# Layer 1's output projection split over heads: three heads' share moved among the attention heads, the rest kept behind them

## The chip, the cores and the metric

The kernel runs on one core of a Trainium2 chip. Its engines work side by side, each through its own queue in order: TensorE (PE; its weight loads are listed as PEld), VectorE (DVE), ScalarE (ACT), GpSimd (POOL) and SyncE (SP), the last of which only issues transfers (DMAs); GpSimd issues some too. The metric is the device time of one launch in microseconds: the median of several runs, and beside it one execution under the profiler, whose trace is quoted.

## What is computed

One inference step of a two-layer decoder trunk: 1024 prompt tokens (16 meta tokens ahead of them) and 8 running sequences of one token each. Layer 0 is a gated linear attention, layer 1 a differential attention over 8 heads; an MLP with squared ReLU follows each, and each result goes through a LayerNorm with a scaled residual. This document is about the end of layer 1's attention. In the reference, cut to that:

```python
def diff_core(q, k, v, q_pos, k_pos, lam):
    s = jnp.einsum('bqhmd,bkhmd->bhmqk', q, k).astype(F32) * (DIFF_DH ** -0.5)
    ...
    p = jax.nn.softmax(s, axis=-1)
    a = p[:, :, 0] - lam * p[:, :, 1]
    return jnp.einsum('bhqk,bkhe->bqhe', a, v.astype(F32))

def diff_output(o, g_sub, lam_init, w_out, dtype):
    B, T = o.shape[:2]
    o = rms_norm(o, g_sub) * (1.0 - lam_init)
    return o.reshape(B, T, DIFF_HEADS * DIFF_DV).astype(dtype) @ w_out

# in reference(), per layer
x_p = post_norm(x_p, f_p, ln_mix_g[layer], ln_mix_b[layer])   # LayerNorm of ALPHA * x + f
x_p = post_norm(x_p, sq_relu_mlp(x_p, mlp_w1[layer], mlp_w2[layer]), ln_mlp_g[layer], ln_mlp_b[layer])
```

The product with w_out sums over the 8 heads (1024 = 8 x 128), so it can be made in parts: some heads first, the others later, and both added to the residual.

## The kernel before

All float32 products of full size are made as three float32r matmuls (`mm3`, profile lines L186 to L188): each operand is split into a high part and the rest (`hi`, `lo`), and hi*hi, hi*lo and lo*hi are summed in PSUM. A weight is loaded into a buffer `raw`, its high part is made on ACT (L173) and the rest on POOL (L174). PSUM is used through three groups of buffers: `mmt` (3), `axt` (3) and `smt` (2).

Layer 1's attention is a loop over 8 heads, and in each over 8 tiles of 128 query rows. `prep(h + 1)` is issued with the first tile of head h: it loads keys, queries and values of the next head (SP), transposes them (PE, L1134 to L1144), splits them (ACT L182, DVE L183) into `XH.t` and `XL.t` of that head's parity, and moves halves between partitions with nine DMAs on POOL's queue (L1150 to L1156). `tile_` makes the scores of both maps (PE L1178 and L1179 into `mmt`; for head 0 L1174 to L1176), masks them and takes the minimum (DVE L1182), takes exps (ACT L1184), combines the two maps (DVE L1186 to L1188), transposes the result (PE L1197 into `axt`), copies it to SBUF as `aT` (ACT L1199, six buffers) and multiplies it with the values (PE L1202 into `smt`). The combined scores of a tile live in `as`, five buffers of the pool `scp`. After four tiles the outputs are copied to `Y` (L1237). `o_norm` scales finished heads (power L1213 on POOL, product L1214 on POOL or DVE).

`o_fm(h, c)` transposes a head's normalized output for rows 512c to 512c + 511 and splits it into `XH[:, h]` and `XL[:, h]` (PE L1220, ACT L1221, DVE L1222). As `XH.t` and `XL.t` hold keys and queries until the last heads, all sixteen `o_fm` come in or behind head 7: half 0 after its first four tiles (rows 0 to 511 come first there), half 1 after its last. `Y` is then loaded again from `xres` in DRAM, where the residual waits (L1261, eight DMAs on SP's queue).

`w_out` (L882) multiplies with layer 1's output weight: four units of 256 columns (`kunit`, whose buffers `whi` and `wlo` the heads use for loaded keys and values), for each half of the rows, in tiles of 2 x 128 rows and 8 heads: 2 x 8 x 3 = 48 matmuls of 128x256 a tile, 16 tiles. DVE adds each tile to `Y` (L900). The samples' part runs beside it (`samples`, issued with the fifth tile): one power on POOL (L1307), 16 products with weights loaded through five buffers `rw` (PE L506). `normalize` follows each row as soon as it is complete, and the MLP of layer 1 takes the result; its weights come through `raw`, `rw` and `RW`.

The order in which the instructions stand in each queue is set by a scheduler that works out a timeline of its own from the program and gives earlier code precedence: an instruction that is ready can be set ahead of one that is not.

Of the kernel before, what the change touches and what calls it, by code (L numbers as in the profile page):

```python
# [11 lines left out]
F32 = mybir.dt.float32  # L12
F32R = mybir.dt.float32r
# [3 lines left out]
ALU = mybir.AluOpType  # L17
# [4 lines left out]
P = 128  # L22
# [6 lines left out]
GH = 4  # L29
FF = 4096  # L30
NPG = 32
ALPHA = 4.0 ** 0.25
EPS = 1e-5
NEG = -1e30
# [76 lines left out]
def hybrid_step(ctx, tc, A, dbg=None, upto=9):  # L111
# [4 lines left out]
    def bc(ap, shape, axis):  # L116
        return ap.unsqueeze(axis).broadcast_to(shape)
# [761 lines left out]

    def w_out(w, scaled, side=None):  # L882

        units = {}
        n = 0
        for u, c in ((0, 0), (1, 0), (0, 1), (1, 1), (2, 0), (3, 0), (2, 1), (3, 1)):
            if u not in units:
                units[u] = kunit(w, u * 256)
            hv, lv = (x.rearrange("p (k n) -> p k n", n=256) for x in units[u])
            for i2 in range(2):  # L890
                ps = mmt()
                t0 = 4 * c + 2 * i2
                for i in range(2):
                    a = slice((t0 + i) * P, (t0 + i + 1) * P)
# [4 lines left out]
                if scaled:  # L899
                    V.tensor_tensor(yv, yv, pv, op=ALU.add)  # L900
                else:
                    steps_v.append(V.scalar_tensor_tensor(yv, yv, ALPHA, pv, ALU.mult, ALU.add).ins)
                if side and (n == 4 if scaled else n < 12):
# [128 lines left out]
    normalize(w_out(A["gla_w_out"][0], False, paged), stats, lambda c: to_fm(c, 0))  # L1032
    normalize(mlp(paged), stats, lambda c: to_fm(c, 1))
    e.close()
    if upto == 2:
# [56 lines left out]


    de.close()
    e = ExitStack()
    a1 = e.enter_context(tc.tile_pool(name="a1", bufs=1))
    a2 = e.enter_context(tc.tile_pool(name="a2", bufs=4))
    a3 = e.enter_context(tc.tile_pool(name="a3", bufs=6))
    scp = e.enter_context(tc.tile_pool(name="scp", bufs=5))
    CW = 448  # L1100
    cm = a1.tile([P, CW], F32, name="cmask")
    V.memset(cm[:, : CW - P], 0.0)
# [110 lines left out]
        G.tensor_tensor(r, r, bc(mhalf[:, :n], [P, n, m], 2), op=ALU.pow)  # L1213
        eng.tensor_tensor(Yd[:, ts, hs], Yd[:, ts, hs], bc(r, [P, n, m, P], 3), op=ALU.mult)  # L1214

    def o_fm(h, c):
        cs = slice(512 * c, 512 * c + 512)
        ps = axt()
        for i in range(4):
            TE.transpose(ps[:, i * P : (i + 1) * P], Yt[:, 4 * c + i, h * P : (h + 1) * P], ident)  # L1220
        S.activation(XH[:, h, cs], ps, AF.Copy, scale=gs)  # L1221
        V.scalar_tensor_tensor(XL[:, h, cs], ps, gs, XH[:, h, cs].bitcast(F32), ALU.mult, ALU.subtract)  # L1222
# [28 lines left out]
    e.close()  # L1251


# [10 lines left out]
    HF = hp.tile([P, NB, 2, TH], F32, name="HF")  # L1264

    RX = hp.tile([P, 4 * TH], F32, name="RX")
    RW = hp.tile([P, 4, 512], F32, name="RW")
# [31 lines left out]

    def samples():  # L1300

        oq = hp.tile([P, 8, NS], F32, name="zoq")
        V.tensor_tensor(oq, oT, oT, op=ALU.mult)
        ps = smt()
        TE.matmul(ps[:, :64], one, oq.rearrange("p h b -> p (h b)"), start=True, stop=True)
        V.tensor_scalar(oq.rearrange("p h b -> p (h b)"), ps[:, :64], 1.0 / P, EPS, ALU.mult, ALU.add)
        G.tensor_tensor(oq, oq, bc(mhalf, [P, 8, NS], 1), op=ALU.pow)  # L1307
        V.tensor_tensor(oq, oq, oT, op=ALU.mult)
        soT = hp.tile([P, NB, TS], F32, name="zoT")
        V.memset(soT, 0.0)  # L1310
        V.tensor_scalar(soT[:, :, NM : NM + NS], oq, gs, None, ALU.mult)
# [260 lines left out]
```

## Time and profile before

| | us |
|---|---|
| median of 3 runs | 2902.23 (2901.81 to 2903.02) |
| the profiled execution | 2897.76 |
| its span, first to last instruction | 2896.0 |
| mean granted TensorE clock | 0.981 |

In the trace head 3 of layer 1 begins at about 1898 us and the last value product of head 7 starts at 2064.3 us; the additions of w_out (L900) run from 2061.7 to 2170.5 us. Rows of the view by windows read: the window in us, its length, then busy us and number of instructions for PE, PEld, DVE, ACT and POOL, then the granted TensorE clock, the DMA engines' share and GB/s. Rows of groups read: line, engine, operation, out<-in, shapes, count, busy us and mean ns of one, then the engine's idle time just before such instructions and what ended it. Rows of the timeline read: start, duration, engine, line, operation and count, and in brackets the idle time before. A matmul's duration includes its way through the pipeline, so that those of neighbours overlap.

### The profile page before, as it was taken

How to read it: one execution, taken by the hardware profiler on the slowest of the kernel's cores; microseconds unless marked ns; L12 is line 12 of the kernel's file. 1: busy time of each engine (PE TensorE's matmuls, PEld its weight loads, DVE VectorE, ACT ScalarE, POOL GpSimd, SP SyncE). 2: the span in 40 equal slices, each digit the busy share in tenths (PEclk: the TensorE clock that was granted, in tenths of full speed). 3: DMA queues.
4: the chain of work that ended last, by engine and by line, in shares of the span. 5: the costliest groups of instructions: out<-in, count | busy, mean ns of one | idle time of the engine just before them, and what ended most of it. 6: DMA issues, size and time to landing. Idle time of an engine off the chain costs nothing. (4 is left out here: it accounts for less than half of the span.)

```text
span 2896.0 us, 52075 instructions
## 1 busy us (share of the span) xinstructions
PE 2773.3 (96%) x19653; PEld 2267.4 (78%) x19653; DVE 1882.9 (65%) x2982; ACT 1043.5 (36%) x2075; POOL 1132.4 (39%) x867
## 2 busy tenths in 40 slices
PE   8889999999999999999999999989998999999997
PEld 5666767997777777777798988888988888797985
DVE  2565544567878777778768822888538846738378
ACT  3233444252221221221231112777424535345352
POOL 1231212234333433333333321122426766777664
PEclk9899999999999999999999998999999999999998
DMA  7557651624798898898668995463447678695894
GB/s 250 181 176 261 245 177 39 231 73 145 268 350 299 301 351 303 321 323 310 254 225 302 363 341 142 101 137 82 120 132 220 174 220 222 160 287 119 258 240 88
DMA packets 285366, 636.46 MB, mean 220 GB/s; under 512 B 25510, under 2 KB 141292, under 8 KB 273852
## 3 DMA queue, kind: packets, MB, share of 16 engines
q1 hardware_dynamic: 252716, 520.66, 52.4%
q0 software_dynamic: 32400, 112.50, 16.2%
q8 instruction: 154, 2.52, 0.4%
q14 instruction: 96, 0.79, 0.1%
HBM read 575.55 MB, written 44.06 MB: 214 GB/s over the span
## 5 line engine op out<-in xcount | busy, mean ns | idle before, releaser
L174 POOL TENSOR_TENSOR wlo<-raw,whi 128x512 fp32r<-128x512 f32 x256 | 357.1, 1408 | 730.1 <-ACT whi L173 635.8
L186 PE MATMUL mmt<-whi,XH 128*128 128x256 f32 (+1 forms) x1760 | 526.1, 300 | 2.2 <-ACT Y L310 2.0
L187 PE MATMUL mmt<-wlo,XH 128*128 128x256 f32 (+1 forms) x1760 | 525.9, 299 | 0.9 <-POOL wlo L174 0.9
L186 PE MATMUL mmt<-XH,whi 128*128 128x512 f32 (+1 forms) x1216 | 436.5, 360 | 7.0 <-DVE HL L183 6.6
L188 PE MATMUL mmt<-whi,XL 128*128 128x256 f32 x1536 | 436.6, 285 | 0.5 <-DVE XL L183 0.5
L188 PE MATMUL mmt<-XH,wlo 128*128 128x512 f32 (+1 forms) x1216 | 434.3, 358 | 0.0
L173 ACT CAST whi<-raw 128x512 fp32r<-128x512 f32 x256 | 153.1, 619 | 579.5 <-PE mmt L188 206.3
L187 PEld LDWEIGHTS mmt<-wlo,XH 128*128 128x128 f32 x1760 | 332.2, 189 | 30.9 <-issue 19.0
L186 PEld LDWEIGHTS mmt<-whi,XH 128*128 128x128 f32 x1760 | 331.5, 189 | 28.2 <-issue 13.5
L790 DVE TENSOR_REDUCE sc<-pg 128x16 f32<-128x1024 f32 x256 | 309.5, 1214 | 62.5 <-POOL pg L789 59.3
L187 PE MATMUL mmt<-XL,whi 128*128 128x512 f32 x768 | 307.3, 400 | 0.0
L188 PEld LDWEIGHTS mmt<-whi,XL 128*128 128x128 f32 x1536 | 289.8, 189 | 13.5 <-issue 11.8
L789 DVE TENSOR_TENSOR pg<-pg,qb 128x1024 f32<-128x1024 f32 x192 | 263.7, 1375 | 53.4 <-DMA pg<-in_cache_k 38.2
L789 POOL TENSOR_TENSOR pg<-pg,qb 128x1024 f32<-128x1024 f32 x64 | 158.8, 2482 | 297.9 <-DMA pg<-in_cache_k 182.4
L186 PEld LDWEIGHTS mmt<-XH,whi 128*128 128x128 f32 x1216 | 230.6, 190 | 54.8 <-issue 14.6
L188 PEld LDWEIGHTS mmt<-XH,wlo 128*128 128x128 f32 x1216 | 231.0, 190 | 38.1 <-issue 5.9
L187 PE MATMUL mmt<-wlo,HH 128*128 128x512 f32 x512 | 204.7, 400 | 0.0
L188 PE MATMUL mmt<-whi,HL 128*128 128x512 f32 x512 | 204.6, 400 | 0.0
L186 PE MATMUL mmt<-whi,HH 128*128 128x512 f32 x512 | 204.4, 399 | 0.0
L187 PEld LDWEIGHTS mmt<-XL,whi 128*128 128x128 f32 x768 | 145.5, 190 | 38.3 <-issue 7.1
L1416 POOL TENSOR_TENSOR wlo<-RW,whi 128x512 fp32r<-128x512 f32 x96 | 156.7, 1762 | 37.1 <-ACT whi L1415 37.1
L1416 POOL TENSOR_TENSOR wlo<-rw,whi 128x512 fp32r<-128x512 f32 x92 | 148.8, 1690 | 43.3 <-ACT whi L1415 43.2
(441 smaller groups left out, 5745.6 us busy)
## 6 DMA issues: line engine op xcount, KB each, us to landing
pg<-in_cache_k SPq DMA_DIRECT2D x256, 512.0 KB
pg<-in_cache_v SPq DMA_DIRECT2D x256, 512.0 KB
XH<-xc POOLq DMA_DIRECT2D x42, 1032.0 KB, 8.7
raw<-in_mlp_w SPq DMA_DIRECT2D x164, 256.0 KB
swt<-in_mlp_w SPq DMA_DIRECT2D x32, 1024.0 KB
rw<-in_mlp_w SPq DMA_DIRECT2D x116, 256.0 KB
RW<-in_mlp_w POOLq DMA_DIRECT2D x96, 256.0 KB, 6.1
xc<-XH POOLq DMA_DIRECT2D x14, 1032.0 KB, 7.6
```

What stands on the lines that cost most here:

```text
L173: S.copy(hi[:, c], raw)
L174: G.tensor_tensor(lo[:, c], raw, hi[:, c].bitcast(F32), op=ALU.subtract)
L186: TE.matmul(ps, ah, bh, start=first, stop=False)
L187: TE.matmul(ps, ah, bl, start=False, stop=False)
L188: TE.matmul(ps, al, bh, start=False, stop=last)
L789: eng.tensor_tensor(pg, pg, qb, op=ALU.mult)
L790: return V.tensor_reduce(sc[:, n, :], pg.rearrange("p (h d) -> p h d", d=64), op=ALU.add, axis=AX.X).ins
L1416: G.tensor_tensor(lo[:, k, :], t, hi[:, k, :].bitcast(F32), op=ALU.subtract)
```

## The change

w_out of layer 1 is made in two parts. Heads 0 to 2 (`EH = 3`): a generator `early_out` issues, one step at a time, `o_fm` of these heads into tiles of their own (`OH`, `OL`), and then for each of the four column units and each pair of row blocks a tile of 2 x 3 x 3 = 18 matmuls, whose result ACT copies into an `aT` buffer and POOL's queue adds to `xres` in DRAM with an accumulating DMA. Its weights lie in a part of `XL.t` that the heads leave free. Steps are taken in heads 2 to 7: four in each of heads 2 to 6, two in head 7. Heads 3 to 7 remain for `late_out`, 2 x 5 x 3 = 30 matmuls a tile, for each half of the rows all four units; the weights of the first three units are split during head 7 (`late_weights`), two of them into the places of `OH` and `OL`. The reloads of `Y` from `xres` go to POOL's queue. The samples' normalization moves to the end of head 1 (`samples_in`). `as` has four buffers where it had five, and the MLP's tile `HF` is allocated only after w_out, in the place of `OH` and `OL`.

```diff
+EH = 3
...
-    scp = e.enter_context(tc.tile_pool(name="scp", bufs=5))
+    scp = e.enter_context(tc.tile_pool(name="scp", bufs=4))
...
-    def o_fm(h, c):
+    def o_fm(h, c, hi=None, lo=None):
         cs = slice(512 * c, 512 * c + 512)
+        if hi is None:
+            hi, lo = XH[:, h - EH, cs], XL[:, h - EH, cs]
...
+    def reload(c):
+        for u in range(4):
+            nc.gpsimd.dma_start(Yt[:, 4 * c : 4 * c + 4, u * 256 : (u + 1) * 256], A["xres"][512 * c : 512 * c + 512, u * 256 : (u + 1) * 256].rearrange("(t p) n -> p t n", p=P))
+    OH = ep.tile([P, EH, T], F32R, name="OH")
+    OL = ep.tile([P, EH, T], F32R, name="OL")
+    wv_ = [x.rearrange("p a n -> p (a n)")[:, 3088 : 3088 + 256 * EH] for x in XL.t]
+    def halves_of(hi, lo, k0, u):
+        for x in range(0, hi.shape[1], 512):
+            w = min(512, hi.shape[1] - x)
+            raw = wrp.tile([P, 512], F32, name="raw")
+            dma(raw[:, :w].rearrange("p (k n) -> p k n", n=256), wo[:, k0 + x // 256 : k0 + (x + w) // 256, u * 256 : (u + 1) * 256])
+            S.copy(hi[:, x : x + w], raw[:, :w])
+            G.tensor_tensor(lo[:, x : x + w], raw[:, :w], hi[:, x : x + w].bitcast(F32), op=ALU.subtract)
+    def out_tile(xh, xl, w, nk, t0):
+        hv, lv = (x.rearrange("p (k n) -> p k n", n=256) for x in w)
+        ps = mmt()
+        for i in range(2):
+            a = slice((t0 + i) * P, (t0 + i + 1) * P)
+            for k in range(nk):
+                mm3(ps[:, i * 256 : (i + 1) * 256], xh[:, k, a], xl[:, k, a], hv[:, k, :], lv[:, k, :], k == 0, k == nk - 1)
+        return ps
+    def early_out():
+        halves_of(*wv_, 0, 0)
+        for h in range(EH):
+            for c in range(2):
+                cs = slice(512 * c, 512 * c + 512)
+                o_fm(h, c, OH[:, h, cs], OL[:, h, cs])
+                yield
+        for u in range(4):
+            for t0 in range(0, 8, 2):
+                ps = out_tile(OH, OL, wv_, EH, t0)
+                o = a3.tile([P, 4, P], F32, name="aT").rearrange("p j q -> p (j q)")
+                S.copy(o, ps)
+                nc.gpsimd.dma_start(A["xres"][t0 * P : (t0 + 2) * P, u * 256 : (u + 1) * 256].rearrange("(i p) n -> p i n", p=P), o.rearrange("p (i n) -> p i n", n=256), accum_op=ALU.add)
+                if t0 == 6 and u < 3:
+                    halves_of(*wv_, 0, u + 1)
+                yield
+    def late_weights():
+        u = len(late_w)
+        if u in (1, 2):
+            x = (OH, OL)[u - 1].rearrange("p k t -> p (k t)")
+            w = x[:, :LW], x[:, LW : 2 * LW]
+        else:
+            w = [wsp.tile([P, 2048], F32R, name=x)[:, :LW] for x in ("whi", "wlo")]
+        halves_of(*w, EH, u)
+        late_w.append(w)
...
             if n == 3 and h == 7:
                 o_norm(V, slice(0, 4), slice(7, 8))
-                for j in range(8):
+                for j in range(EH, 8):
                     o_fm(j, 0)
-        if h < 6 and h % 2:
-            o_norm(G, slice(0, 8), slice(h - 1, h + 1))
-        elif h == 6:
-            o_norm(G, slice(0, 8), slice(6, 7))
+                reload(0)
+            if h == 2 and n < 4 or h == 3 and n in (0, 2, 4, 6) or 3 < h < 7 and n % 2 == 0 or h == 7 and n < 2:
+                next(early)
+            if h == 7 and n in (1, 2, 4):
+                late_weights()
+        if h == 1:
+            soT = samples_in()
+        if h in (1, 2, 4, 6):
+            o_norm(G, slice(0, 8), slice(2 if h == 2 else h - 1, h + 1))
     o_norm(V, slice(4, 8), slice(7, 8))
-    for j in range(8):
+    for j in range(EH, 8):
         o_fm(j, 1)
+    reload(1)
...
-    for c in range(2):
-        for u in range(4):
-            dma(Yt[:, 4 * c : 4 * c + 4, u * 256 : (u + 1) * 256], A["xres"][512 * c : 512 * c + 512, u * 256 : (u + 1) * 256].rearrange("(t p) n -> p t n", p=P))
...
-    normalize(w_out(A["diff_w_out"][0], True, samples()), stats, lambda c: to_fm(c, 2, xr))
+    def late_out():
+        side, n = samples(), 0
+        late_weights()
+        for c in range(2):
+            for u in range(4):
+                for t0 in (4 * c, 4 * c + 2):
+                    ps = out_tile(XH, XL, late_w[u], NB - EH, t0)
+                    yv = Yt[:, t0 : t0 + 2, u * 256 : (u + 1) * 256]
+                    V.tensor_tensor(yv, yv, ps.rearrange("p (i n) -> p i n", n=256), op=ALU.add)
+                    if n == 4:
+                        next(side)
+                    n += 1
+                    if u % 2:
+                        for t in (t0, t0 + 1):
+                            yield t, u // 2
+    normalize(late_out(), stats, lambda c: to_fm(c, 2, xr))
```

What this makes of the order, at two places. First TensorE's queue at the beginning of head 4, where the last transposes of head 5's preparation and the scores of head 4 stand. Before, scores (L1178, L1179), transposes of the combined scores (L1197) and value products (L1202) follow them:

```order
L1144 MATMUL axt<-c_ident,wlo 128x128 x4
L1178 MATMUL mmt<-XH_83 128x464
L1179 MATMUL mmt<-XH_83,XL_85 128x464
L1197 MATMUL axt<-c_ident,as 128x128 x4
L1178 MATMUL mmt<-XH_83 128x448
L1179 MATMUL mmt<-XH_83,XL_85 128x448
L1197 MATMUL axt<-c_ident,as 128x128 x5
L1202 MATMUL smt<-vm_20991,aT 128x128
L1202 MATMUL smt<-whi,aT 128x128 x3
```

Now, at the same place, in the numbering of the changed kernel, where L187 to L189 are the three matmuls of `mm3`:

```order
L1144 MATMUL axt<-c_ident,wlo 128x128 x4
L1178 MATMUL mmt<-XH_83 128x384
L1179 MATMUL mmt<-XH_83,XL_85 128x384
L187 MATMUL mmt<-XL_85,OH 128x256
L188 MATMUL mmt<-XL_86,OH 128x256
L189 MATMUL mmt<-XL_85,OL 128x256
L187 MATMUL mmt<-XL_85,OH 128x256
L188 MATMUL mmt<-XL_86,OH 128x256
L189 MATMUL mmt<-XL_85,OL 128x256
```

Of the 18 rows of that tile of early_out the first six are shown; the others follow in the same manner, without a row of the heads between them, and three more such blocks stand further back in the head.

Second, GpSimd's queue in head 4, where the moves of head 5's keys and queries stand. Before:

```order
L1154 DMA XL_86<-XL_86 64x1024
L1155 DMA XL_86<-XL_86 64x1024
L1214 TENSOR_TENSOR Y<-Y,orr 128x8x256
L1151 DMA XH_84<-XL_86 64x1040
L1156 DMA XH_84<-XH_84 64x1024
L1156 DMA XL_86<-XL_86 64x1024
```

Now (L1243 splits weights of early_out, L1267 is the accumulating DMA, L1228 the reload of `Y`):

```order
L1154 DMA XL_86<-XL_86 64x1024
L1155 DMA XL_86<-XL_86 64x1024
L1243 TENSOR_TENSOR XL_86<-raw,XL_85 128x512
L1151 DMA XH_84<-XL_86 64x1040
L1243 TENSOR_TENSOR XL_86<-raw,XL_85 128x256
L1267 DMA xres<-aT 128x2x256
L1156 DMA XH_84<-XH_84 64x1024
L1156 DMA XL_86<-XL_86 64x1024
L1267 DMA xres<-aT 128x2x256
L1228 DMA Y<-xres 128x4x256
L1267 DMA xres<-aT 128x2x256 x2
```

Weight splits, accumulating DMAs and a reload now stand between and behind the moves; the product L1214 that stood here is elsewhere.

More of the change, by code (lines that the diff above doesn't have):

```diff
@@ L878, in hybrid_step, with w_out @@
                 split(XH[:, 2 * h + m, cs], XL[:, 2 * h + m, cs], fmv[:, h, c, m, :])
-    def w_out(w, scaled, side=None):
+    def w_out(w, side):
         units = {}
@@ L898, in w_out @@
                 pv = ps.rearrange("p (i n) -> p i n", n=256)
[L899 to L903, printed above, removed]
+                steps_v.append(V.scalar_tensor_tensor(yv, yv, ALPHA, pv, ALU.mult, ALU.add).ins)
+                if n < 12:
                     next(side)
@@ L1031, in hybrid_step @@
     paged = decode()
-    normalize(w_out(A["gla_w_out"][0], False, paged), stats, lambda c: to_fm(c, 0))
+    normalize(w_out(A["gla_w_out"][0], paged), stats, lambda c: to_fm(c, 0))
     normalize(mlp(paged), stats, lambda c: to_fm(c, 1))
@@ L1094, in hybrid_step @@
     de.close()
+    ee = ExitStack()
+    ep = ee.enter_context(tc.tile_pool(name="ep", bufs=1, side="right"))
     e = ExitStack()
@@ new lines, in hybrid_step @@
+    OH = ep.tile([P, EH, T], F32R, name="OH")
+    OL = ep.tile([P, EH, T], F32R, name="OL")
+    wo = A["diff_w_out"][0].rearrange("(k p) n -> p k n", p=P)
+    wv_ = [x.rearrange("p a n -> p (a n)")[:, 3088 : 3088 + 256 * EH] for x in XL.t]
[6 more added lines that the diff above has]
+            G.tensor_tensor(lo[:, x : x + w], raw[:, :w], hi[:, x : x + w].bitcast(F32), op=ALU.subtract)
@@ new lines, in hybrid_step, with samples_in @@
+    LW = 256 * (NB - EH)
+    late_w = []
+    def late_weights():
[7 more added lines that the diff above has]
+        late_w.append(w)
+    def samples_in():
+        oq = ep.tile([P, 8, NS], F32, name="zoq")
+        V.tensor_tensor(oq, oT, oT, op=ALU.mult)
+        ps = smt()
+        TE.matmul(ps[:, :64], one, oq.rearrange("p h b -> p (h b)"), start=True, stop=True)
+        V.tensor_scalar(oq.rearrange("p h b -> p (h b)"), ps[:, :64], 1.0 / P, EPS, ALU.mult, ALU.add)
+        G.tensor_tensor(oq, oq, bc(mhalf, [P, 8, NS], 1), op=ALU.pow)
+        V.tensor_tensor(oq, oq, oT, op=ALU.mult)
+        soT = ep.tile([P, NB, TS], F32, name="zoT")
+        V.memset(soT, 0.0)
+        V.tensor_scalar(soT[:, :, NM : NM + NS], oq, gs, None, ALU.mult)
+        return soT
@@ L1225, in hybrid_step @@
+    early = early_out()
     nxt = prep(0)
@@ L1300, in samples @@
     def samples():
[L1302 to L1311, printed above, removed]
         s_post(s_rows(soT, A["diff_w_out"][0], NB), 2, hp)
@@ L1315, in hybrid_step @@
     stats = ln_stats(hp)
-    normalize(w_out(A["diff_w_out"][0], True, samples()), stats, lambda c: to_fm(c, 2, xr))
+    def late_out():
[14 more added lines that the diff above has]
+    normalize(late_out(), stats, lambda c: to_fm(c, 2, xr))
+    ee.close()
+    fp = e.enter_context(tc.tile_pool(name="fp", bufs=1))
+    HF = fp.tile([P, NB, 2, TH], F32, name="HF")
     if upto == 4:
```

5 lines of the change are left out of this document (2 added, 3 removed).

## The prediction

> **What bounds the kernel now.** I read the page's busy line first, then the stretches around the last layer-1 heads, then single instructions.
>
> ```profile
> PE 2773.3 (96%) x19653; PEld 2267.4 (78%) x19653; DVE 1882.9 (65%) x2982; ACT 1043.5 (36%) x2075; POOL 1132.4 (39%) x867
> ```
>
> 96% for TensorE is an average over stages. The windows by stage (busy us per engine, counts in brackets, then clock, DMA share, GB/s) separate them: two whole heads, the end of head 7, and the three pieces of w_out behind it.
>
> ```profile
> 1931.00:1961.00 30.00, 26.57 (x198) 23.37 (x197) 26.36 (x78) 21.15 (x53) 11.16 (x11) 1.00 0.63 133
> 1961.00:1993.00 32.00, 29.97 (x215) 27.64 (x215) 27.82 (x99) 24.28 (x58) 4.59 (x9) 0.95 0.40 93
> 2042.60:2064.60 22.00, 21.62 (x183) 21.02 (x184) 10.94 (x23) 9.43 (x19) 1.01 (x1) 1.00 0.20 62
> 2064.60:2104.70 40.10, 39.40 (x335) 39.15 (x333) 16.57 (x28) 9.32 (x16) 22.83 (x13) 1.00 0.55 150
> 2104.70:2131.10 26.40, 26.40 (x133) 14.19 (x131) 2.66 (x4) 3.09 (x5) 7.51 (x6) 1.00 0.61 187
> 2131.10:2171.30 40.20, 40.20 (x343) 40.20 (x343) 22.58 (x53) 15.52 (x20) 8.53 (x9) 1.00 0.30 101
> ```
>
> From 2042.6 to 2171.3 TensorE is busy 127.6 of 128.7 us while VectorE works 52.8. All of w_out lies there (3 x 256 = 768 records), and VectorE's additions wait for it:
>
> ```profile
> L186 PE MATMUL mmt<-whi,XH 128*128 128x256 f32 x256 | 72.4, 286 | 0.2 <-ACT XH L1221 0.2
> L187 PE MATMUL mmt<-wlo,XH 128*128 128x256 f32 x256 | 72.4, 284 | 0.0
> L188 PE MATMUL mmt<-whi,XL 128*128 128x256 f32 x256 | 72.2, 285 | 0.0
> ...
> L900 DVE TENSOR_TENSOR Y<-Y,mmt 128x512 f32<-128x512 f32 x16 | 11.0, 685 | 48.1 <-PE mmt L188 48.1
> ```
>
> In the heads both engines look 85 to 90% busy, but a matmul's 284 ns overlap its neighbours. What one costs is the distance between starts:
>
> ```profile
> 2079.11 0.28 PE L186 MATMUL mmt<-whi,XH 128*128 128x256 f32 x1
> 2079.23 0.28 PE L187 MATMUL mmt<-wlo,XH 128*128 128x256 f32 x1
> 2079.34 0.28 PE L188 MATMUL mmt<-whi,XL 128*128 128x256 f32 x1
> ...
> 1901.27 0.34 PE L1178 MATMUL mmt<-XH 128*128 128x400 f32 x1
> 1901.45 0.35 PE L1179 MATMUL mmt<-XH,XL 128*128 128x400 f32 x1
> ...
> 1914.22 1.28 PE L1202 MATMUL smt<-whi,aT 128*128 128x128 f32 x10
> 1915.34 0.93 PE L1197 MATMUL axt<-c_ident,as 128*128 128x128 f32 x7
> ```
>
> A w_out matmul takes 0.117 us, a 400-column score 0.18 us, a value product (1.28 - 0.28) / 9 = 0.111 us, a transpose (0.93 - 0.27) / 6 = 0.110 us. Head 4's counts (window 1931 to 1961):
>
> ```profile
> L1202 PE MATMUL smt<-whi,aT 128*128 128x128 f32 x76 | 10.6, 275 | 0.0
> L1178 PE MATMUL mmt<-XH 128*128 128x400 f32 (+9 forms) x22 | 8.0, 380 | 0.0
> L1179 PE MATMUL mmt<-XH,XL 128*128 128x400 f32 (+9 forms) x22 | 6.8, 326 | 0.0
> L1197 PE MATMUL axt<-c_ident,as 128*128 128x128 f32 x44 | 6.6, 276 | 2.7 <-DVE as L1188 2.3 <-DVE XL L183 0.4
> L1202 PE MATMUL smt<-vm,aT 128*128 128x128 f32 x17 | 3.6, 289 | 0.2 <-ACT aT L1199 0.2
> ```
>
> 93 x 0.111 + 44 x 0.110 + 44 scores x 0.15 (mean width 338 columns, scaled from 0.18) + 17 prep transposes x 0.11 = 10.3 + 4.8 + 6.6 + 1.9 = 23.6 us. So a head of 30 us leaves TensorE some **6.4 us** truly free, and the tail leaves none. The free time isn't spread evenly:
>
> ```profile
> 1900.00:1905.00 5.00, 4.55 (x31) 3.92 (x31) 4.94 (x19) 4.82 (x14) 0.22 (x1) 1.00 0.41 122
> 1905.00:1910.00 5.00, 2.96 (x13) 1.88 (x12) 5.00 (x18) 2.67 (x6) 2.83 (x6) 0.93 1.22 277
> 1910.00:1915.00 5.00, 5.00 (x32) 4.83 (x31) 4.84 (x17) 4.09 (x11) 0.73 (x2) 0.73 1.28 224
> 1915.00:1920.00 5.00, 5.00 (x45) 5.00 (x44) 3.45 (x12) 3.85 (x10) 0.79 (x2) 1.00 0.82 152
> ...
> 1970.00:1975.00 5.00, 4.26 (x17) 3.69 (x18) 5.00 (x16) 2.62 (x7) 2.05 (x4) 0.66 1.00 224
> ...
> 2000.00:2005.00 5.00, 4.61 (x22) 3.84 (x21) 5.00 (x17) 2.95 (x7) 4.06 (x4) 0.66 0.28 57
> ```
>
> Early in a head VectorE is full (5.00 of 5) and TensorE runs 13 to 32 matmuls, at times at a lower clock; later TensorE runs 45, one per 0.11 us, and is the bound.
>
> **The change, part by part.** *Out of the tail:* 16 tiles x 2 x 3 heads x 3 = 288 matmuls x 0.117 = 33.7 us, and six o_fm (24 transposes x 0.110 = 2.6 us). Since TensorE sets the end there, **-36.3 us**. The 16 additions, the sample products and LayerNorm stay. The tail now does all four column units of rows 0 to 511 before rows 512 to 1023, so LayerNorm of the first half has 8 tiles x 30 x 0.117 = 28 us of matmuls beside it, where it had 4 x 48 x 0.117 = 22 us: no new wait there. HF, allocated later in the place of OH and OL, is first written by the MLP, after their last read.
>
> *Into the heads:* the same 36.3 us. By the calls: 1.8 in head 2 (four o_fm), 5.1 in head 3 (two o_fm, two tiles), 8.4 in each of heads 4 to 6 (four tiles), 4.2 in head 7. Per head 4 to 6 that exceeds the free 6.4 us, so at best 2.0 us each stay visible. At worst all 8.4 do: the order shows a tile as one block of 18, 2.1 us, in line with the scores, and the score tiles have 4 buffers where they had 5, so VectorE is sometimes left dry behind a block. I take 3.7 us hidden per head: the one block straight behind prep's transposes stands where VectorE is full (2.1), the other three where TensorE is already dense, some 0.5 each (chosen between 0 and 6.4). With 3.3 hidden in head 3, 1.2 in head 2 and 1.5 in head 7, 17.1 of 36.3 us vanish and **+19.2 us** show.
>
> *ACT, DVE:* 16 copies of 128x512 at the aT copy's 0.58 us, 2.3 us a head, and twelve o_fm pairs moved. ACT has 8 us idle a head, VectorE gains idle time as heads stretch: nothing on the path while TensorE leads.
>
> ```profile
> L1199 ACT COPY aT<-axt 128x512 f32<-128x512 f32 x64 | 36.7, 581 | 27.7 <-PE axt L1197 27.4
> ...
> L1307 POOL TENSOR_TENSOR zoq<-zoq,mhalf 128x64 f32<-128x64 f32 x1 | 10.6, 10569 | 1.4 <-DVE zoq L1306 1.4
> ...
> 1875.08 0.51 POOL L1150 DMA_DIRECT2D XH<-XH  x1 [17.06 <-ACT XH L182]
> ```
>
> The 10.6 us power of samples() goes from the tail, where w_out covered it, to GpSimd ahead of the moves that head 2 issues for head 3. Before those GpSimd sat idle for 17.1 us (the row of 1875.08), which covers it; without that cover the moves, and head 3, would be up to 10.6 us late.
>
> *GpSimd's queue:* 16 accumulating DMAs and 8 reloads join the prep moves.
>
> ```profile
> 1897.60 0.33 SPq L1125 DMA_DIRECT2D vm<-out_v_rows_p  x1
> ...
> 1904.78 0.51 POOL L1150 DMA_DIRECT2D XH<-XH  x1 [14.02 <-ACT XH L182]
> ...
> 1912.46 0.51 POOL L1151 DMA_DIRECT2D XH<-XL  x1 [3.91 <-DMA XH<-XH]
> ...
> 1918.03 0.51 POOL L1156 DMA_DIRECT2D XL<-XL  x1 [2.74 <-DMA XL<-XL]
> ...
> 2084.73 0.86 POOL L1414 DMA_DIRECT2D RW<-in_mlp_w  x1 [0.91 <-DMA RW<-in_mlp_w]
> ...
> RW<-in_mlp_w POOLq DMA_DIRECT2D x4, 256.0 KB, 6.1
> ```
>
> The vm load marks head 3's start. The moves end 20 us into a head (1918.0 - 1897.6). An accumulate queued behind them starts at 21, takes 0.9 to issue and 6.1 to land: 28 us. Until then it holds one of six aT buffers, which the head's value products share; a later ACT copy on that buffer, 23 to 28 us into a head, waits 0 to 5 us, and the exps behind it too. A reload also waits for its accumulates, but behind it stand moves due in the next head. Bounds 0 and 15 us over three heads, taken **+3**.
>
> The Trainium skill's page DMA: Bandwidth & Descriptors ("Anatomy of one DMA") gives a GpSimd-issued DMA 2.0 us plus bytes / 436 GB/s, an estimate of 2.6 us for 256 KB. By it these waits vanish and the sum is 3 us better; this trace's 6.1 us differs, and no row has an accumulate into DRAM, so the row is used.
>
> *Head of the tail:* the first five sample weights now follow the last head by some 8 us of matmuls (60 x 0.117 and twelve transposes), not 40. Five loads of 256 KB and three reloads of 512 KB, 2.9 MB, take 11 us at the 277 GB/s of the window from 1905 and 15 at the 187 of this stretch: 3 to 7 us if nothing of it starts earlier, nothing if the loads start during head 7's last tiles. Between 0 and 7 I take **+2**, since the reloads come out on a queue of their own and are needed last. Late weights split earlier and reloads off SP's queue save nothing: TensorE did not wait for them.
>
> Sum: -36.3 + 19.2 + 3 + 2 = **-12.1 us**: span 2896.0 to 2883.9. The profiled run took 2897.8, 4.5 us under the median shown; carried over, 2902.2 - 12.1 = **2890**.
>
> The clock dips where TensorE idles (0.73, 0.66 above): a window at 0.66 loses 1.7 us of work, and there is one such in heads 3, 5 and 6. The Trainium skill's TensorE: Matmul & The Clock Gate ("Part 1: The HAM clock gate") says the clock halves after an idle window and stays full under sustained work. By that rule the inserted blocks would end the dips and the sum would be up to 5 us better, an estimate; the trace agrees that dips sit in the sparse windows. I leave it out.
>
> **Rivals.** (a) *The heads absorb all free time.* For it: 6.4 us free per head. Against: three blocks of four stand in dense stretches. Heads 4 to 6 show 2.0 each, head 7 1.2, no waits: -36.3 + 7.2 = -29, 2873. (b) *Waits eat the gain:* 17.1 hidden, but 8 us of aT waits and 5 for sample weights: -4, 2898. (c) *Slower: GpSimd's queue blocks ACT.* Accumulates behind the moves land at 28 us, aT copies wait 4 to 5 us in each of heads 4 to 6 (14 us), TensorE stands with them, and the blocks hide only 6 us: -6 + 14 = +8, 2910. For it: the queue is in order and ACT too; against: buffers may be reused later than I think. It decides once waits exceed what is hidden. (d) *The move does nothing,* since it never overlaps: hidden 0, no waits, 2902; that is (b)'s side of no change.
>
> **Numbers.** The forecast (-6 to -21) 0.42, (a) 0.18, (b) with (d) 0.17, (c) 0.23. About 0.2%, 5.8 us, is what can be told from no change: faster 0.42 + 0.18 = 0.60, same 0.17, slower 0.23. Range 2873 (a) to 2909 (nearly c); the forecast's own 2881 to 2896.
>
> **What will show it.** w_out behind head 7 should span some 70 us with TensorE full, where it was 107; heads 4 to 6 last 34 to 37 us (over 39: c; 32 to 33: a). ACT's aT copies waiting for xres DMAs over 8 us in sum speak for (b) or (c); idle before the first sample product over 3 us breaks the tail's term. I am wrong at the root if TensorE idles in the tail, or if heads 0 and 1, which get nothing, lengthen through the fifth score buffer's loss.

## The result, and the profile after

The changed kernel takes 2914.0 us (median of 6 runs, 2908.3 to 2919.5), the kernel before 2901.1 (6 runs, 2897.1 to 2903.0): ratio 1.0044, 95% interval 1.0032 to 1.0057. It is slower by 0.4%, where 2890 was forecast and the range ended at 2909. The nearest time among the rivals was (c)'s 2910, but its mechanism isn't what happened.

The page of the changed kernel, its busy line:

```profile
PE 2779.1 (95%) x19653; PEld 2273.4 (78%) x19653; DVE 1873.0 (64%) x2982; ACT 1057.2 (36%) x2095; POOL 1174.5 (40%) x895
```

The windows by stage (columns as in the prediction), first of the kernel before: from the first score of head 0 to the last value product of head 7, then to the last transpose behind LayerNorm, then the MLP.

```profile
1790.90:2064.40 273.50, 250.72 (x1762) 224.85 (x1763) 221.39 (x713) 189.38 (x446) 62.08 (x76) 0.94 0.50 113
2064.40:2187.00 122.60, 120.39 (x925) 107.23 (x923) 51.46 (x100) 36.91 (x55) 48.94 (x37) 1.00 0.51 152
2187.00:2896.00 709.00, 666.38 (x4087) 573.87 (x4084) 476.02 (x587) 303.54 (x563) 473.63 (x403) 0.98 0.74 198
```

The same three stages of the changed kernel, and its heads 3, 4 and 5 (from one `vm` load to the next):

```profile
1790.80:2120.50 329.70, 296.43 (x2069) 267.99 (x2070) 231.99 (x722) 207.81 (x476) 111.22 (x110) 0.92 0.55 118
2120.50:2207.50 87.00, 84.00 (x618) 70.88 (x617) 45.12 (x90) 29.74 (x43) 28.59 (x29) 1.00 0.61 190
2207.50:2915.50 708.00, 665.50 (x4087) 574.62 (x4085) 470.22 (x587) 304.37 (x563) 471.88 (x403) 0.98 0.73 198
...
1910.50:1950.50 40.00, 36.55 (x267) 33.43 (x266) 28.87 (x89) 25.64 (x59) 11.56 (x14) 0.96 0.59 116
1950.50:1991.10 40.60, 36.83 (x283) 33.86 (x282) 28.84 (x95) 27.25 (x63) 12.82 (x16) 1.00 0.73 158
1991.10:2030.10 39.00, 37.37 (x278) 34.75 (x278) 25.92 (x85) 26.25 (x61) 18.26 (x17) 0.96 0.58 113
```

The tail behaves as forecast: 122.6 us became 87.0, 35.6 less (the term was 36.3), and the MLP is untouched. All of the loss is in the heads: 273.5 us became 329.7, 56.2 more for 36.3 us of moved TensorE work. TensorE there is busy 45.7 us longer, idle 10.5 us longer (329.7 - 296.4 against 273.5 - 250.7), and the granted clock fell from 0.94 to 0.92. VectorE was busy 81% of that stage before and is 70% now (221.4 of 273.5 us, 232.0 of 329.7). Its waits for scores there, of the kernel before (us in total, times, longest):

```profile
DVE as L1182 <- PE mmt L1179: 16.8, 20, 3.9
```

and of the changed kernel:

```profile
DVE as L1182 <- PE mmt L1179: 39.7, 35, 4.8
```

The two profiled executions differ by 19.5 us, the medians by 12.9: the same kernel before gave 2891.9 to 2911.2 in 29 runs made together. So below, profiles tell where time goes, and medians how much.

The timeline of the changed kernel shows what hangs on a block of 18 matmuls. Here are the first and last matmul of two blocks, the two waits of VectorE for scores and the two copies:

```profile
1947.80 0.39 PE L187 MATMUL mmt<-XL,OH 128*128 128x256 f32 x1
...
1949.92 0.28 PE L189 MATMUL mmt<-XL,OL 128*128 128x256 f32 x1
...
1957.76 0.38 PE L187 MATMUL mmt<-XL,OH 128*128 128x256 f32 x1
...
1959.86 0.28 PE L189 MATMUL mmt<-XL,OL 128*128 128x256 f32 x1
...
1961.31 0.44 DVE L1182 CUSTOM_DVE_ANT_0 as<-mmt,cmask 128x272 f32<-128x272 f32 x1 [0.68 <-PE mmt L1179]
...
1962.75 0.60 ACT L1266 COPY aT<-mmt 128x512 f32<-128x512 f32 x1
...
1965.92 0.44 DVE L1182 CUSTOM_DVE_ANT_0 as<-mmt,cmask 128x272 f32<-128x272 f32 x1 [1.59 <-PE mmt L1179]
...
1966.19 0.60 ACT L1266 COPY aT<-mmt 128x512 f32<-128x512 f32 x1
```

Each of these blocks takes 2.4 us from its first start to its last end. Its copy starts long after: the first block ends at 1950.2 and is copied at 1962.8, the second ends at 1960.1 and is copied at 1966.2. The scores use the same three `mmt` buffers of PSUM, so from 1957.8 to 1963.3 one of three was left to them. ACT's queue is in order, and ahead of such a copy stand `aT` copies whose transposes TensorE makes only after the block. That VectorE's waits come from this held buffer is a theory so far; e3 below tests it.

### The profile page after: what moved, and what is told of

Same layout as the page of the kernel before. It is cut to its first block, busy times and chain, and to the rows that moved or that the text cites. A ratio compares the mean times of both kernels' runs of the same rounds, so it can differ in the third digit from the quotient of the medians.

```text
span 2915.5 us, 52147 instructions
## 1 busy us (share of the span) xinstructions
PE 2779.1 (95%) x19653; PEld 2273.4 (78%) x19653; DVE 1873.0 (64%) x2982; ACT 1057.2 (36%) x2095; POOL 1174.5 (40%) x895
## 4 chain that ended last, share of the span: by engine, by line
PE 71%; DMA 10%; DVE 10%; issue 5%; POOL 2%; ACT 1%; SPq 0%; DVEq 0%; POOLq 0%; ACTq 0%
PE mmt L187 17%; PE mmt L188 17%; PE mmt L189 16%; PE smt L831 4%; PE axt L187 2%; PE axt L188 2%; PE axt L189 2%; PE smt L1202 2%; DMA XH<-xc 1%; DMA rw<-in_mlp_w 1%; DMA swt<-in_mlp_w 1%; PE axt L1197 1%; PE smt L507 1%; DVE pg L790 1%; DVE Y L1577 1%
## 5 line engine op out<-in xcount | busy, mean ns | idle before, releaser
L175 POOL TENSOR_TENSOR wlo<-raw,whi 128x512 fp32r<-128x512 f32 x240 | 346.3, 1456 | 664.4 <-ACT whi L174 591.3
L187 PE MATMUL mmt<-whi,XH 128*128 128x256 f32 (+1 forms) x1584 | 478.0, 302 | 4.1 <-DVE ast L1182 2.1
L188 PE MATMUL mmt<-wlo,XH 128*128 128x256 f32 (+1 forms) x1584 | 477.5, 302 | 0.8 <-POOL wlo L175 0.8
L187 PE MATMUL mmt<-XH,whi 128*128 128x512 f32 (+1 forms) x1216 | 436.3, 360 | 6.6 <-DVE HL L184 6.4
L189 PE MATMUL mmt<-XH,wlo 128*128 128x512 f32 (+1 forms) x1216 | 433.6, 357 | 0.0
L189 PE MATMUL mmt<-whi,XL 128*128 128x256 f32 x1360 | 388.4, 287 | 0.0
L174 ACT CAST whi<-raw 128x512 fp32r<-128x512 f32 x240 | 143.5, 620 | 526.3 <-PE mmt L189 205.7
L187 PEld LDWEIGHTS mmt<-whi,XH 128*128 128x128 f32 x1584 | 300.1, 190 | 30.5 <-issue 13.5
L188 PEld LDWEIGHTS mmt<-wlo,XH 128*128 128x128 f32 x1584 | 300.5, 190 | 28.9 <-issue 17.7
L187 PEld LDWEIGHTS mmt<-XH,whi 128*128 128x128 f32 x1216 | 230.5, 190 | 54.1 <-issue 14.1
L189 PEld LDWEIGHTS mmt<-whi,XL 128*128 128x128 f32 x1360 | 258.1, 190 | 11.0 <-issue 10.1
L189 PEld LDWEIGHTS mmt<-XH,wlo 128*128 128x128 f32 x1216 | 230.5, 190 | 37.9 <-issue 5.9
L189 PE MATMUL mmt<-whi,HL 128*128 128x512 f32 x512 | 204.6, 400 | 0.0
L187 PE MATMUL mmt<-whi,HH 128*128 128x512 f32 x512 | 204.4, 399 | 0.0
```

The costliest lines, as they stand in the source:

```text
L174: S.copy(hi[:, c], raw)
L175: G.tensor_tensor(lo[:, c], raw, hi[:, c].bitcast(F32), op=ALU.subtract)
L187: TE.matmul(ps, ah, bh, start=first, stop=False)
L188: TE.matmul(ps, ah, bl, start=False, stop=False)
L189: TE.matmul(ps, al, bh, start=False, stop=last)
```

## The experiments

Each run was timed together with the kernel before on the same chip. The numbers are medians; the difference is to the median of the kernel before in the runs made with it. Where two of these differences are subtracted below, the result is uncertain by some 5 to 10 us; runs of different groups are compared through the kernel before.

| run | us | difference | ratio, 95% interval |
|---|---|---|---|
| the change | 2914.0 | +12.9 | 1.0044 [1.0032, 1.0057] |
| e1_before_scp4 | 2901.9 | -0.8 | 0.9998 [0.9984, 1.0012] |
| e2_after_scp5 | 2914.6 | +11.9 | 1.0042 [1.0021, 1.0062] |
| e3_after_axt | 2906.4 | +3.7 | 1.0006 [0.9994, 1.0018] |
| e4_after_noaccum | 2911.2 | +8.5 | 1.0028 [1.0010, 1.0045] |
| e5_none | 2873.1 | -31.1 | 0.9888 [0.9870, 0.9907] |
| e6_third | 2897.8 | -6.5 | 0.9987 [0.9972, 1.0002] |
| e7_axt_samples_back | 2907.9 | +3.6 | 1.0014 [1.0001, 1.0027] |
| e8_axt_samples_norms | 2909.7 | +5.5 | 1.0023 [1.0010, 1.0037] |
| e9_half_tiles | 2912.4 | +10.2 | 1.0029 [1.0014, 1.0044] |
| e10_o_fm_only | 2874.0 | -28.1 | 0.9895 [0.9867, 0.9923] |
| e11_axt_norms | 2902.1 | 0.0 | 0.9994 [0.9975, 1.0012] |
| e12_axt_third | 2896.8 | -5.4 | 0.9978 [0.9964, 0.9992] |
| e13_before_dummy | 2922.4 | +20.5 | 1.0076 [1.0053, 1.0099] |
| e14_before_dummy_copy | 2927.4 | +25.5 | 1.0087 [1.0062, 1.0111] |
| e15_after_nocopy | 2894.5 | -7.4 | 0.9978 [0.9964, 0.9992] |
| e16_after_nosplit | 2914.1 | +12.2 | 1.0040 [1.0027, 1.0053] |
| e17_axt_norms_vcopy | 2910.5 | +6.1 | 1.0026 [1.0015, 1.0036] |
| e18_mmt_norms_vcopy | 2913.4 | +8.9 | 1.0032 [1.0018, 1.0047] |

**The fifth score buffer.** Heads 0 and 1 of the changed kernel, which hold no moved work, took 83.9 us where 77.0 stood. The first theory, T1, gave this to the buffer.

```diff
 (kernel before)
-    scp = e.enter_context(tc.tile_pool(name="scp", bufs=5))
+    scp = e.enter_context(tc.tile_pool(name="scp", bufs=4))
```

> The kernel before with four score buffers (as) where it has five, nothing else. Theory T1 (the fifth buffer's loss costs every head some 3.4 us, as heads 0 and 1 of the changed kernel show without any moved work: 48.4 and 35.5 us where 45.2 and 31.8 stood): 8 x 3.4 = 27 us slower, 2922 to 2934, heads 1 to 6 at 33 to 37 us. Rival T2 (the loss comes with the moved blocks themselves and the heads 0 and 1 only had a lower clock): 2898 to 2907.

```diff
 (changed kernel)
-    scp = e.enter_context(tc.tile_pool(name="scp", bufs=4))
+    scp = e.enter_context(tc.tile_pool(name="scp", bufs=5))
-    OL = ep.tile([P, EH, T], F32R, name="OL")
+    OL = OH
```

> The changed kernel with five score buffers; room is made by writing the low halves of heads 0 to 2 over the high ones, so the output of w_out's first three heads is another one, while every instruction stays. T1: some 27 us faster than the changed kernel, 2882 to 2892, heads 0 and 1 back at 45 and 32 us. T2: heads 0 and 1 may come back, the rest not: 2908 to 2916.

-0.8 and +11.9: T1 falls from both sides. The buffer's loss costs nothing that can be measured. In e1's profile heads 0 and 1 took 82.9 us as well, although its time is that of the kernel before: a long head in one profile is not yet a loss. Whether the buffer lengthened heads 0 and 1 of the changed kernel isn't shown either way (in e2, with five, they took 80.4).

**The PSUM buffer, and GpSimd's queue.**

```diff
-                ps = out_tile(OH, OL, wv_, EH, t0)
+                ps = out_tile(OH, OL, wv_, EH, t0, axt)      # axt() there in place of mmt()
```

> The changed kernel with the 18-matmul tiles of the early part in the transposes' PSUM buffers (axt) in place of the scores' (mmt), four score buffers kept. Theory T3 (the block holds one of the scores' three PSUM buffers until ACT, behind its exps, copies it, and VectorE runs dry for 1 us a block): 8 to 16 us faster than the changed kernel, 2898 to 2906. T1 alone: 2910 to 2918.

```diff
                 S.copy(o, ps)
-                nc.gpsimd.dma_start(A["xres"]..., accum_op=ALU.add)
```

> The changed kernel without the 16 accumulating DMAs (the first three heads' share of w_out is computed and copied, but not added to the residual). The prediction's rival (c) (accumulates behind the moves on GpSimd's queue hold aT buffers and ACT waits): 10 to 15 us faster, 2899 to 2904. T1: 2910 to 2916, since ACT's aT copies show no wait for a DMA.

With the blocks out of the scores' buffers 9.2 us of the loss are gone (+3.7 for +12.9, and the intervals don't meet). In e3's trace the 16 copies start within 1.4 us of their block's end, and ACT now waits for blocks, 9.2 us in all. But VectorE's waits for scores, which T3 explains the loss by, did not get shorter: 40.3 us where the changed kernel has 39.7. They do not go with the time elsewhere either: e1, as fast as the kernel before, has 30.6, and e5 (below), without any block, 31.0. The rows of e3, e1 and e5:

```profile
DVE as L1182 <- PE mmt L1179: 40.3, 34, 5.0
```

```profile
DVE as L1182 <- PE mmt L1179: 30.6, 28, 4.7
```

```profile
DVE as L1182 <- PE mmt L1179: 31.0, 26, 5.2
```

So the other buffers bring 9.2 us, and that they do so by sparing VectorE these waits is not shown.

Without the accumulating DMAs 4.4 us are gone, with intervals that do meet: nearer the +3 forecast than (c)'s 10 to 15, but not clear of nothing.

**What the blocks cost in all.** Two runs leave the moved work out, wholly and but for its transposes.

```diff
-    early = early_out()
+    early = iter([None] * 22)
```

> The changed kernel with early_out left out: no o_fm, weights, tiles, copies or accumulating DMAs of heads 0 to 2 at all (their share of w_out is missing from the output), everything else as in the change. The heads grew by 56 us in the changed kernel, of which 36.8 us are the moved TensorE work. Theory T4 (the blocks cost their own TensorE time and the other 19 us come with the rest of the change: four score buffers, the samples' power and the splits in new places): 2874 to 2880. Theory T5 (the other 19 us come with the blocks, by lower clock, held buffers and waits): 2856 to 2868.

```diff
 (early_out, behind the six o_fm)
-        for u in range(4):
-            for t0 in range(0, 8, 2):
-                ...
+        yield from [None] * 16
```

> The changed kernel with the early o_fm of heads 0 to 2 (24 transposes, 2.6 us) and the first weight splits, but without the 16 early tiles, their copies, DMAs and later splits (that share of w_out is missing from the output). Without both it was 2873. If o_fm costs its transposes alone: 2874 to 2878. If its wait for GpSimd's product (3.7 us) and what is queued behind it count: 2880 to 2886.

2873.1 lies just under T4's range and above T5's, and the kernel before stood 3 us higher in the runs made with it than in those the expectation went by. Against it the run is at -31.1, where -36.3 would be free of any other cost: the rest of the change costs some 5 us, with an interval from nothing to about 10, and not 19. Where it does isn't settled; in e5's profile (of a run 6.6 us above its median) the heads took 285.6 us without any moved work, where 273.5 stood, at a clock of 0.92:

```profile
1792.30:2077.90 285.60, 252.56 (x1752) 228.20 (x1753) 221.93 (x716) 190.91 (x448) 85.28 (x88) 0.92 0.52 116
```

The early `o_fm` add 3 us by the medians (-28.1), which can't be told from nothing, although in the changed kernel TensorE waits once for GpSimd's product, behind the samples' power:

```profile
1892.06 1.12 PE L1222 MATMUL axt<-c_ident,Y 128*128 128x128 f32 x4 [3.69 <-POOL Y L1214]
```

So the 16 tiles cost some 41 us where their matmuls take 33.7.

**The matmuls, or what hangs on them.** One matmul in place of three, in `mmt` and in `axt`:

```diff
-                mm3(ps[...], xh[:, k, a], xl[:, k, a], hv[:, k, :], lv[:, k, :], ...)
+                TE.matmul(ps[...], xh[:, k, a], hv[:, k, :], ...)
```

> The changed kernel with one matmul in place of three in the early tiles (high by high halves alone, so the first three heads' share of w_out is rounded): 192 matmuls fewer, 22.5 us at 0.117, every copy, DMA and wait kept. If TensorE's time in the heads is all visible: 2889 to 2894. If half of the work is hidden there, as the prediction has it: 2900 to 2906. If the copies, PSUM buffers and DMAs carry the loss and not the matmuls: 2908 or more.

> The one-matmul early tiles (high by high halves alone, 2898) in axt. If the gain of axt is the PSUM buffer's hold and not the matmuls' time, it adds up: 2888 to 2892. If with a third of the matmuls the block (0.7 us) no longer outlasts the scores in store: 2896 to 2899.

192 matmuls fewer bring 19.4 us of their 22.5 (+12.9 to -6.5); the other 96, 11.2 us, with all that hangs on the tiles still cost 21.6 (-28.1 to -6.5). e6 itself, 2897.8, lies between its ranges. In `axt` nothing is added (-5.4), although e6's copies come 3.0 to 11.0 us behind their blocks, as late as in the change, and all but two of e12's within 1.6 us. By e12's expectation that speaks against the held buffer alone: held as long behind short blocks, it costs nothing that shows. e12 is the only version with every part in place that is clearly faster than the kernel before, and it buys that with the precision of three heads' products.

Then bare matmuls of a constant tile `dm` in the kernel before (its w_out stays whole in the tail), without and with a copy:

```diff
 (kernel before, in the places of the 16 early tiles)
+        ps = mmt()
+        for i in range(2):
+            for k in range(9):
+                TE.matmul(ps[:, i * 256 : (i + 1) * 256], dm[:, :P], dm[:, 256:], start=k == 0, stop=k == 8)
+        S.copy(<a buffer of aT>, ps)      # e14 alone
```

> The kernel before, all of its w_out kept in the tail, with 16 added blocks of 18 matmuls of a constant tile in the places of the change's early tiles (two in head 3, four in each of heads 4 to 6, two in head 7), in mmt buffers that nobody reads: 33.7 us of TensorE work and nothing else. Theory T7 (the heads have no free time for blocks): 2902 + 34 = 2934 to 2941. The prediction's step (half hidden): 2915 to 2922.

> The same with ACT copying each block's PSUM buffer into an aT buffer that nobody reads. Theory T3 (the held buffer and the copy cost 0.5 us a block): 6 to 10 us above the run before it. T7 alone: within 3 us of it.

And the changed kernel without copies and DMAs, or without its later weight splits:

```diff
 (e15)
-                o = a3.tile([P, 4, P], F32, name="aT").rearrange("p j q -> p (j q)")
-                S.copy(o, ps)
-                nc.gpsimd.dma_start(A["xres"]..., accum_op=ALU.add)
 (e16)
-                if t0 == 6 and u < 3:
-                    halves_of(*wv_, 0, u + 1)
```

> The changed kernel without the early tiles' copies and accumulating DMAs; the matmuls and weight splits stay (the share of heads 0 to 2 is computed and dropped). Without the DMAs alone it was 2911. T3: 2900 to 2905. If the matmuls alone make the loss: 2909 to 2914.

> The changed kernel with the weights of early_out loaded and split for its first column unit only, and used for all four (the share of heads 0 to 2 is computed with wrong weights). If the splits (six casts on ACT, six subtractions on GpSimd, beside which VectorE waits) cost the path something: 2905 to 2910. If not: 2911 to 2917.

e13 and e15 price the matmuls. 33.7 us of bare matmuls make the kernel before 20.5 us longer (15 to 29); in the changed kernel the 16 tiles without copies cost 20.7 (-28.1 to -7.4, uncertain by 9). Two kernels, one answer: about 13 of 33.7 us hide in the heads, and T7 (nothing hides) falls. With the copies the changed kernel goes from -7.4 to +8.5, 15.9 us (some 9 to 22) for 16 copies that take 9.6 us of ACT. The splits cost nothing that shows (+12.2).

In the kernel before the added copies cost 5 us only, with an interval that reaches from below nothing to about 14 us. Yet they come as late there: 2.3 to 10.7 us behind their blocks, 5.4 on average, where the change has 0.2 to 12.5 and 5.5. Neither e14 nor e15 fell into one of its ranges: e14 lies between them, e15 below both.

The windows over the heads, of e13 and of e15, and VectorE's waits for scores in e15:

```profile
1791.00:2087.20 296.20, 279.79 (x2051) 257.74 (x2051) 221.91 (x713) 190.28 (x446) 61.72 (x76) 0.94 0.47 104
```

```profile
1785.50:2094.20 308.70, 283.39 (x2069) 260.98 (x2070) 231.69 (x722) 197.97 (x460) 89.63 (x94) 0.94 0.49 112
```

```profile
DVE as L1182 <- PE mmt L1179: 26.3, 36, 3.8
```

In e15 the stage is 21 us shorter than in the change (308.7 for 329.7) with the same count of matmuls, the clock is back at 0.94, and VectorE waits 26.3 us for scores where it waited 39.7. These are single profiles, of two runs 25 us apart where the medians differ by 19.

**Repairs that were tried.**

```diff
 (e7, e8: on e3)
-        if h == 1:
-            soT = samples_in()
 (samples)
+        soT = samples_in()
 (e8, e11)
-        if h in (1, 2, 4, 6):
-            o_norm(G, slice(0, 8), slice(2 if h == 2 else h - 1, h + 1))
+        if h in (1, 2, 3, 5, 6):
+            o_norm(G, slice(0, 8), slice(h - 1 if h in (1, 5) else h, h + 1))
```

> As the run with the early tiles in axt (2906), and the samples' normalization back behind the heads, where it was before the change. If its 10.6 us power on GpSimd delays the norm of heads 0 and 1 and so TensorE's transposes (3.7 us of wait for L1214): 2899 to 2904. If w_out in the tail no longer covers it there: 2905 or more.

> As the run before it, and the norms made for heads 0-1, 2, 3, 4-5, 6 in place of 0-1, 2, 3-4, 5-6, so that GpSimd's product in head 7 is 128x1024 (2 us) and not 128x2048 (4.4 us), beside which one VectorE operation took 5.7 us. If that stall and the lower clock behind it make the hole of head 7: 4 to 8 us below the run before it, 2893 to 2898. If not: within 2 us of it.

> As the run with the early tiles in axt (2906), with the norms made for heads 0-1, 2, 3, 4-5, 6, and the samples at the end of head 1 as in the change. The run with the samples moved too had its heads 8.6 us shorter and lost 9 us in w_out behind them to a late LayerNorm. If the shorter heads come from the norms: 2898 to 2902. If they came from the samples: 2904 to 2908.

```diff
 (e9: on e3, 32 blocks of 9 in place of 16 of 18)
-            for t0 in range(0, 8, 2):
-                ps = out_tile(OH, OL, wv_, EH, t0, axt)
+            for t in range(8):
+                ps = axt()[:, :256]
+                ... one row block, its own copy and DMA
```

> As the run with the early tiles in axt (2906), with each tile cut in two: 32 blocks of 9 matmuls (1.05 us), each with its own PSUM buffer, copy and accumulating DMA, one behind every score tile of heads 4 to 6. Theory T6 (a block of 2.1 us outlasts the scores that VectorE has in store, which it eats at about 0.58 us a piece from three buffers, so it runs dry): 4 to 10 us below it, 2896 to 2902. Rival: twice the copies and DMAs cost as much as the shorter blocks bring: 2904 to 2912.

The samples behind the heads bring nothing (+3.6), with the norms +5.5. In e8's profile the heads took 312.1 us for e3's 320.7, and the tail gave it back (97.1 for 87.7); TensorE waited there 5.1 us for LayerNorm's rows, in e3 0.6. The norms alone stand at 0.0, 3.7 below e3 with intervals that meet: not shown. Half blocks did not bring T6's gain (+10.2 for +3.7, with intervals that just meet). As e9 also doubles the copies and DMAs, it doesn't tell the length of a block from their number.

Last, the copy on VectorE, on e11 (`axt`) and in `mmt`:

```diff
-                S.copy(o, ps)
+                V.tensor_copy(o, ps)
```

> As the run with axt and the norms (2902), with the early tiles copied by VectorE in place of ACT. If the late copy is the loss: 2892 to 2898, near the run without copies (2894.5). If VectorE has no room for 16 x 0.6 us: 2902 to 2908.

> The same in the scores' PSUM buffers (mmt), where VectorE's copy stands behind two to seven scores that are made after the block. If the late copy is the loss: between the two, 2896 to 2904. If ACT's time is the loss: as the run before it, within 2 us.

+6.1 and +8.9 where e11 stood at 0.0. In e17 each copy starts within 0.9 us of its block's end, so a prompt copy alone does not bring the time back. A copy on VectorE takes 0.69 us (on ACT in e3 0.59), and these runs don't separate its lateness from the time it takes on either engine.

## Why the prediction was wrong

By the runs, in the order in which the parts were put back:

| part | predicted | measured | from |
|---|---|---|---|
| tail without three heads | -36.3 | -36.3 | taken over; the windows show -35.6 |
| rest of the change | +2 | +5 | e5 |
| early o_fm and matmuls in the heads, as far as they show | +19.2 | +23.7 | e5 to e10 to e15 |
| copies on ACT | 0 | +15.9 | e15 to e4 |
| accumulating DMAs | +3 | +4.4 | e4 to the change |
| sum | -12.1 | +12.9 | |

Each single difference is uncertain by 5 to 7 us, the sum by about 4; what the first row has wrong would stand in the second. Of the other rivals (a), 2873, and (b) and (d), 2898 and 2902, none came: the heads took in a third of the moved work, not all and not nothing.

*The step that failed* is the one on ACT: "16 copies of 128x512 at the aT copy's 0.58 us, 2.3 us a head ... nothing on the path while TensorE leads." This term of the sum, put at nothing, measured 15.9 us in the changed kernel, and it is the only one whose miss is larger than its uncertainty. Its size is not pinned down: in the kernel before the same copies cost 5 us (e14), and the two intervals meet. The duration was right:

```profile
L1266 ACT COPY aT<-mmt x16: 588/603/622, 1937.7 to 2073.7; 128x512 f32<-128x512 f32 x16
```

What the prediction did not look at is when a copy's turn comes: ACT's idle time says that it fits, and over the 16 blocks it came 0.2 to 12.5 us after the block's end, with a PSUM buffer held until then. The prediction did see that VectorE "is sometimes left dry behind a block", but tied it to the score buffers in SBUF (`as`, five to four), which e1 and e2 show to be worth nothing that can be measured, and not to the three PSUM buffers. Blocks in other PSUM buffers, with copies that follow promptly, are 9.2 us faster (e3). The Trainium skill's Perfetto Trace Analysis ("Optimizing Tensor Performance", Matmuls) asks that independent groups rotate through PSUM banks so that the copy of one overlaps the matmuls of the next; the gain of e3 agrees with it.

*How* the copies cost their time stays open. The late copy and its held buffer were the theory, and three things speak against them as the whole cause: VectorE waits for scores as long in e3 as in the change, copies as late cost nothing that shows behind short blocks (e6 against e12), and copies as late cost only 5 us in e14. With prompt copies e3 still stands 11 us above e15, and the DMAs measured 4.4 of them. ACT's own time in front of the exps is a candidate, but no run took that alone.

*Right in mechanism, off in size:* the hidden share. 17.1 of 36.3 us was forecast, 12.6 measured (36.3 - 23.7, uncertain by 7), and e13 gives 13 of 33.7 in another kernel. That part of the work hides, and not all, is shown. The size came near partly by luck: the 3.7 us a head were chosen between 0 and 6.4, and no run tells in which blocks the work hid. The rest of the change was sized at 2 (the sample weights, which measured 1.3 us of idle) and came to 5, which its interval doesn't tell from 2. One working behind the 2 is slightly off: 2.9 MB at 277 GB/s are 10.4 us, not 11.

*Right within the noise, not for the reason given:* the accumulating DMAs. No `aT` copy of the changed kernel waited for one; ACT's longest waits in the stage are for VectorE and TensorE:

```profile
ACT as L1184 <- DVE ast L1182: 50.0, 49, 7.2
ACT aT L1199 <- PE axt L1197: 41.8, 34, 5.8
ACT Y L1312 <- PE smt L1202: 7.8, 6, 2.9
```

So rival (c), accumulates that hold `aT` buffers, was wrong though its 2910 was near. What the DMAs cost, if anything, has no cause shown. They landed so (median, in us):

```profile
xres<-aT POOLq DMA_DIRECT2D x16, 256.0 KB, 5.0
```

That lies between the trace's 6.1 and the 2.6 worked out from the Trainium skill's DMA: Bandwidth & Descriptors; the row was the better guide.

*The clock.* By the rule of the Trainium skill's TensorE: Matmul & The Clock Gate the blocks might have ended the dips. They didn't: 0.94 before, 0.92 after. Nor are they shown to have lowered the clock: e5 has 0.92 without any block, e13 0.94 with bare ones. TensorE's longest idle stretch in the heads is one in head 7 (4.5 us, at 2080; the last section shows it), and dips stand there and behind it:

```profile
2070.00:2080.00 10.00, 9.14 (x61) 7.34 (x58) 6.60 (x27) 8.62 (x22) 8.76 (x7) 1.00 0.52 94
2080.00:2090.00 10.00, 5.48 (x24) 5.03 (x23) 8.32 (x14) 4.44 (x9) 5.52 (x4) 0.66 0.27 92
2090.00:2100.00 10.00, 6.56 (x33) 5.02 (x32) 10.00 (x24) 7.22 (x15) 6.93 (x6) 0.81 0.34 119
```

*The signs that were named* helped in part. w_out behind head 7 took 70.6 us, to the end of its last addition, where some 70 were forecast, and TensorE idle in the tail, which would have broken the root, stayed at 3 us. Heads 3 to 5 took 39 to 41 us: over 39 was named as the sign of (c), and it came with another cause. Heads 0 and 1 did lengthen in the profile, but the fifth score buffer, named as the reason, costs no time that shows.

## What to carry to other kernels

Work moved into another stage brings its evacuation (the copy out of PSUM) with it, and the copy's duration and its engine's idle time don't price it: here 9.6 us of copies cost 15.9. Look up what stands ahead of the copy in its engine's queue and whose PSUM buffers the block holds until then, and price it by a run without it. When a theory names a wait, look whether that wait shrinks in the run that helps; here it didn't. Free time of the bound engine can be measured directly, by putting the bare matmuls there with nothing hanging on them; here 13 of 33.7 us hid, and that was known only after e13. When a loss is split over runs that differ by 4 us, put the parts back one by one and use medians: runs of one kernel, and so their profiles, differed by more than most parts (19.3 us over 29 runs).

## What the runs showed of the hardware

One VectorE operation on 128x144 took 5.69 us, where the shortest of its line takes 0.36 (least, median and greatest duration in ns), while GpSimd split weights and then ran a product of 128x2048, and TensorE, waiting for it, stood still for 4.5 us (lines of VectorE, GpSimd and TensorE in the changed kernel's timeline):

```profile
L1188 DVE SCALAR_TENSOR_TENSOR as<-as,ast x64: 362/898/5690, 1806.9 to 2102.9; 128x1040 f32<-128x1040 f32 x8, 128x272 f32<-128x272 f32 x8, 128x784 f32<-128x784 f32 x8, 128x528 f32<-128x528 f32 x8
```

```profile
2079.03 5.69 DVE L1188 SCALAR_TENSOR_TENSOR as<-as,ast 128x144 f32<-128x144 f32 x1
```

```profile
2080.19 4.36 POOL L1214 TENSOR_TENSOR Y<-Y,orr 128x2048 f32<-128x2048 f32 x1
```

```profile
2084.78 0.69 PE L1197 MATMUL axt<-c_ident,as 128*128 128x128 f32 x2 [4.52 <-DVE as L1188]
```

It ends 0.2 us behind GpSimd's product. The Trainium skill's SBUF — State Buffer ("SBUF: two separate sides") says that a VectorE operation with two SBUF inputs and a GpSimd operation that reads SBUF lock each other out for a whole instruction; the trace agrees in that it ended with the product, though here it outlasted a split as well. The kernel before has such stalls too, up to 4.39 us beside a product, so by itself it doesn't explain the loss. This one fell where TensorE had nothing else, and the lower clock of the rows above came with it.
